# Norm sums and rows in one product each, and the mLSTM's diagonal and first states moved by a step

## The chip, the cores and the metric

The kernel runs on one core of a Trainium2 chip. The metric is the device time of one execution in microseconds (us). The kernel before takes 884.66 us, the median of three runs (884.0 to 885.25).

## The reference

One layer of a hybrid encoder on 512 tokens of 1024 channels, with 256 memory tokens, in float32:

```python
h = rms_norm(x, mix_norm_g)                      # y = x * rsqrt(mean(x*x) + EPS) * g
proj = h @ w_in                                  # mLSTM q,k,v,o,gates | NA q,k,v | memory q | merge gates
y_ml = mlstm_branch(...)                         # 4 heads of 128, chunkwise, forward and backward scans
y_na = neighbourhood_attention(...)              # 8 heads of 64 on an 8 x 64 grid
mem_k, mem_v = split(rms_norm(mem, mem_norm_g) @ w_mem_kv)
y_xa = memory_cross_attention(...)               # 4 heads of 128
merged = g_ml*(y_ml @ w_br_ml) + g_na*(y_na @ w_br_na) + g_xa*(y_xa @ w_br_xa)
x = x + merged @ w_out
a, u = split(rms_norm(x, ffn_norm_g) @ w_ffn_up) # ConvGLU, 2816 wide
x = x + (gelu(dwconv3(a)) * u) @ w_ffn_down
out = rms_norm(x, final_norm_g)
```

## The kernel before

Channels lie on the partitions and tokens along the free axis, so a projection of 128 output channels is a 128x512 tile that sums over 8 input tiles (k = 0 to 7). A float32 factor is kept as a high part in fp32r and a low part (the remainder), and `mm3` issues three products for each k: high x high, high x low, low x high (L203 to L205). A projection (`proj`) is therefore 24 products into one PSUM bank; `at={k: f}` lets it call `f` after the products of that k. Weights come in by `wr` loads on SP (L151), and ACT and DVE split them (L185, L186) ahead of their use. All engines work through their own instructions in order.

The norm factors `1/rms` are applied after the projections. The sum of squares of a token runs over partitions, so it is a product with a matrix of ones (`onesr`). `rstd_parts` splits the squares into a high and a low part (ACT L209, DVE L210); `rstd_cols` multiplies each by the ones into one bank (two products, L291), takes the diagonal of each 128 columns (L295) and raises it to -1/2 on POOL (L298). That gives a column `rc`: one number for each token, on partitions. `rstd_row` makes the same numbers a row `rb` on all partitions: the column, split in high and low (L300, L301), scales the identity (L306, one for each 128 tokens and part), and two products with the ones (L314) spread it. This happens for the norm of x, of the memory ("m", 256 tokens) and of the FFN ("2"); the final norm has no row.

The mLSTM is a generator whose pieces are put between the projections by hand: each `yield` hands back to the projections, which resume it once or twice a projection. Its start (`ml_prep`) makes gates, scans, a small diagonal matrix `dg` (L544) that spreads the scans' maxima (L551), and the tables `R` (loaded by SP from DRAM at L576; `load_R` also adds a mask on DVE, L579, giving `rm`). For a head, `begin` transposes keys (L598, L600) and scales them (ACT L602, DVE L604), `middle` computes the chunk states (L641, copied at L644 and combined at L646) and the first half of the decay matrices (`diagonal`: ACT exponentials of `rm` at L614, DVE L618), `rest` the second half, and `last` the weighted queries (L628, L630) and `load_R` of the next head. `values_J` (L657, L659) gives the outputs of a head in four parts, with the next head's `begin`, `middle`, `rest` and `last` behind them.

The projections around the first head are mLSTM's o0 to o3 (bank read by DVE L976, ACT L977, DVE L980), then the memory's keys and values. The memory norm's sums are issued in o2 after k=3, its row in the first key projection. In the FFN, `ua` and `uu` are the two halves of the up-projection; the sums of norm 2 are issued in `ua1`, its row behind it.

Of the kernel before, what the change touches and what calls it, by code (L numbers as in the profile page):

```python
# [11 lines left out]
F32 = mybir.dt.float32  # L12
F32R = mybir.dt.float32r
AF = mybir.ActivationFunctionType
ALU = mybir.AluOpType
AX = mybir.AxisListType

P = 128
S = 512
D = 1024  # L20
# [82 lines left out]
def hybrid_block(ctx, tc, xT, memT, wflat, vecs, gbias, nabias, outa, outb):  # L103
    nc = tc.nc
    V, A, G, PE, SY = nc.vector, nc.scalar, nc.gpsimd, nc.tensor, nc.sync

    cp = ctx.enter_context(tc.tile_pool(name="cp", bufs=1))
    wp = ctx.enter_context(tc.tile_pool(name="wp", bufs=3))
    up = ctx.enter_context(tc.tile_pool(name="up", bufs=NU))
    sp = ctx.enter_context(tc.tile_pool(name="sp", bufs=7))  # L110
    tp = ctx.enter_context(tc.tile_pool(name="tp", bufs=2))
# [6 lines left out]
    def nm(s):  # L118
        uid[0] += 1
        return f"{s}_{uid[0]}"  # L120
# [4 lines left out]
    def scr(n=512):  # L125
        return sp.tile([P, 512], F32, tag="scr", name=nm("s"))[:, :n]

    def tiny(n):
        return tp.tile([P, 32], F32, tag="tiny", name=nm("y"), bufs=12)[:, :n]
# [4 lines left out]
    def atps():  # L134
        return atp.tile([P, 512], F32, tag="at", name=nm("at"))
# [71 lines left out]
    def split_act(h, l, src, scale=1.0):  # L207

        A.activation(h, src, AF.Copy, scale=scale)  # L209
        V.scalar_tensor_tensor(l, src, scale, h.bitcast(F32), op0=ALU.mult, op1=ALU.subtract)  # L210
# [40 lines left out]

    ident = cp.tile([P, P], F32, name="ident")
    make_identity(nc, ident)
    ones = cp.tile([P, P], F32, name="ones")
    G.memset(ones, 1.0)
    onesr = cp.tile([P, P], F32R, name="onesr")
# [4 lines left out]
    for d in range(2):  # L261
# [4 lines left out]
                        pattern=[[sgn, P]], channel_multiplier=-sgn)  # L266
        msk.append(m)
    pads = []
    for i in range(2):
        t = cp.tile([P, 514], F32, name=f"pad{i}")  # L270
# [8 lines left out]

    def rstd_parts(acc, ntok):  # L280

        h, l = [sp.tile([P, 512], F32R, tag="scr", name=nm("s"))[:, :ntok] for _ in range(2)]
        split_act(h, l, acc)
        return h, l

    def rstd_cols(parts, ntok, tag, n=D):

        nt = ntok // P
        ps = atps()
        for i, part in enumerate(parts):  # L290
            PE.matmul(ps[:, :ntok], onesr, part, start=i == 0, stop=i == 1)  # L291
        v = tiny(nt)
        d = scr(P)
        for t in range(nt):
            V.tensor_tensor_reduce(d, ps[:, t * P:(t + 1) * P], ident, 1.0 / n, EPS, ALU.mult, ALU.add,  # L295
                                   accum_out=v[:, t:t + 1])
        col = cp.tile([P, nt], F32, name=f"rc_{tag}")
        G.tensor_tensor(col, v, nhalf[:, :nt], op=ALU.pow)  # L298
        ch, cl = tp.tile([P, 32], F32R, tag="tiny", name=nm("y"), bufs=12)[:, :nt], tiny(nt)
        A.activation(ch, col, AF.Copy)  # L300
        V.tensor_tensor(cl, col, ch.bitcast(F32), op=ALU.subtract)  # L301
        dgs = []
        for c in (ch.bitcast(F32), cl):
            dg = sp.tile([P, 512], F32R, tag="scr", name=nm("s"))[:, :ntok]
            for t in range(nt):
                V.tensor_scalar(dg[:, t * P:(t + 1) * P], ident, c[:, t:t + 1], None, op0=ALU.mult)  # L306
            dgs.append(dg)
        return col, dgs

    def rstd_row(dgs, ntok, tag):  # L310

        pb = atps()
        for n, dg in enumerate(dgs):
            PE.matmul(pb[:, :ntok], onesr, dg, start=n == 0, stop=n == 1)  # L314
        rb = cp.tile([P, ntok], F32, name=f"rb_{tag}", tag=f"rb{ntok}", bufs=2 if ntok == S else 1)
        A.activation(rb, pb[:, :ntok], AF.Copy)
        return rb
# [3 lines left out]
    XH = [hx[k // 4][:, (k % 4) * S:(k % 4 + 1) * S] for k in range(KT)]  # L321
    XL = [hx[2 + k // 4][:, (k % 4) * S:(k % 4 + 1) * S] for k in range(KT)]
    acc = cp.tile([P, S], F32, name="acc_x", tag="acc", bufs=1)
# [19 lines left out]
    norm = []  # L343

    def proj(key, XHs, XLs, n=S, bank=None, at={}):
        ws = weights(key)
        ps = (bank or mmps)()
        for k in range(KT):
            mm3(ps[:, :n], ws[k][0], ws[k][1], XHs[k], XLs[k], k == 0, k == KT - 1)
            if k in at:  # L350
                at[k]()
        return ps
# [3 lines left out]
    for k in range(KT):  # L356
# [6 lines left out]
        for f in range(4):  # L363
            fs = slice(f * P, (f + 1) * P)
            mm3(ps_q[f], wh[:, fs], wl[:, fs], XH[k], XL[k], k == 0, k == KT - 1)

    xp = rstd_parts(acc, S)
    ps_k = [proj(("mlk", 0), XH, XL, bank=atps, at={3: lambda: norm.append(rstd_cols(xp, S, "x"))}),
            proj(("mlk", 1), XH, XL, bank=atps, at={3: lambda: norm.append(rstd_row(norm[0][1], S, "x"))})]
    (rc, _), rb = norm  # L370
    rcc = cp.tile([P, NT], F32, name="rcc")
    V.tensor_scalar(rcc, rc, C_ML, None, op0=ALU.mult)
# [22 lines left out]
    for f in range(4):  # L395
        ps = ps_k[f] if f < 2 else proj(("mlk", f), XH, XL)
# [42 lines left out]
    for c, n in enumerate(TMW):  # L439
# [9 lines left out]
        for t in range(NT):  # L449
            ps = pss[t]  # L450
# [21 lines left out]
    ml = {}  # L472


    def ml_prep(load_R):
        gv = Gt.rearrange("p t (d k h) -> p t d k h", d=2, k=2)
        T4 = lambda a: a.rearrange("p (t d h) -> p t d h", t=4, d=2)
        f = tiny(32)
# [50 lines left out]
        dg = cp.tile([P, 4, NT, 4], F32, name="dg")  # L529
# [4 lines left out]
        for d in range(2):  # L534
            G.dma_start(rd[d], rr[32 * d:32 * d + 4, :])
        ml["rd"] = rd
        yield
        ml["R"] = load_R(0)
        for d in range(2):
            for u in range(2):  # L540
                g = 2 * u + d
                gs = slice(32 * g, 32 * g + 4)
                ends = mr[gs].rearrange("p (t c) -> p t c", t=NT)[:, :, P - 1 if d == 0 else 0:][:, :, 0:1]
                V.tensor_tensor(dg[gs, g], ends.to_broadcast([4, NT, 4]),  # L544
                                ident[gs, gs].unsqueeze(1).to_broadcast([4, NT, 4]), op=ALU.mult)
        pm = atps()
        pmv = pm[:, :400].rearrange("p (t c) -> p t c", t=NT)
        for t in range(NT):
# [20 lines left out]
    def ml_all():  # L569
# [125 lines left out]
        def begin(h):  # L695
            kt, C = own(h)
            st_[h] = dict(kt=kt, C=C, kq=keys(h, kt), R=ml.pop("R"))
# [14 lines left out]
                ml["R"] = load_R(h + 1)  # L712

        begin(0)
        yield
        middle(0)
        yield
# [4 lines left out]
        for h in range(4):  # L722
            x = st_.pop(h)
# [242 lines left out]
    for f in range(4):  # L966
        ps = proj(("xaq", f), XH, XL, at=mid())
# [3 lines left out]
    for f in range(4):  # L971
# [3 lines left out]
        t = scr()  # L975
# [26 lines left out]
    for f in range(4):  # L1002
        ps = proj(("naq", f), XH, XL, at=mid())
        V.tensor_tensor(nq[:, f * S:(f + 1) * S].rearrange("p (b r c) -> p b r c", r=ROWS, b=4), rv(ps), rv(rb),
                        op=ALU.mult)
# [201 lines left out]
    for hh in range(2):  # L1207
        gu = [unit(F32R) for _ in range(6)]
        UH = [gu[k // 4][:, (k % 4) * S:(k % 4 + 1) * S] for k in range(HF)]
        UL = [gu[3 + k // 4][:, (k % 4) * S:(k % 4 + 1) * S] for k in range(HF)]  # L1210
        for j in range(HF):
            f = HF * hh + j
            if f == 0:
                wa, wu = weights(("ua", f)), weights(("uu", f))
                pa, pu = mmps(), mmps()
                for k in range(KT):
                    if k < KT - 1:
                        mm3(pa, wa[k][0], wa[k][1], HH[k], HL[k], k == 0, False)
                for k in range(KT - 1):
                    mm3(pu, wu[k][0], wu[k][1], HH[k], HL[k], k == 0, False)  # L1220
                p2 = rstd_parts(acc2, S)
                k = KT - 1
                mm3(pa, wa[k][0], wa[k][1], HH[k], HL[k], False, True)
                mm3(pu, wu[k][0], wu[k][1], HH[k], HL[k], False, True)
            else:
                pa = pa1 if f == 1 else proj(("ua", f), HH, HL)
            if f == 0:
                pa1 = proj(("ua", 1), HH, HL, at={0: lambda: norm.append(rstd_cols(p2, S, "2"))})
                rb2 = rstd_row(norm[4][1], S, "2")
            c = conv(pa, rb2, "ffw", "ffb", f, FT)  # L1230
            sq = scr()
            A.activation(sq, c, AF.Square)
            V.scalar_tensor_tensor(sq, sq, GC, c, op0=ALU.add, op1=ALU.mult)  # L1233
            A.activation(sq, sq, AF.Tanh, scale=GK)  # L1234
            V.scalar_tensor_tensor(c, sq, 1.0, c, op0=ALU.add, op1=ALU.mult)  # L1235
            G.tensor_tensor(c, c, rb2, op=ALU.mult)  # L1236
            if f > 0:
                pu = proj(("uu", f), HH, HL)
            V.tensor_tensor(c, pu, c, op=ALU.mult)  # L1239
            split_act(UH[j], UL[j], c, 0.5)  # L1240
        for f in range(KT if hh == 0 else LF - 1):
            ws = weights(("dn", hh, f, 0)) + weights(("dn", hh, f, 1))
            ps = mmps()
            for k in range(HF):
                mm3(ps, ws[k][0], ws[k][1], UH[k], UL[k], k == 0, k == HF - 1)
            V.tensor_tensor(x2[f], ps, x2[f], op=ALU.add)
            if hh == 1:
                if f == 0:
                    A.activation(acc3, x2[f], AF.Square)
                else:  # L1250
                    sq = scr()
                    A.activation(sq, x2[f], AF.Square)
                    G.tensor_tensor(acc3, acc3, sq, op=ALU.add)
                A.activation(x2[f], x2[f], AF.Copy, scale=vcol("fin_g", f))
        if hh == 1:
            last_tiles(UH, UL)
# [107 lines left out]
```

## Time and profile before

| | |
|---|---|
| median of three runs | 884.66 us (884.0 to 885.25) |
| the profiled execution | 883.28 us, of which the span is 881.5 us |
| instructions | 12183 |
| PE busy | 874.1 us, 4330 products |
| DVE, ACT, POOL busy | 581.7, 449.7, 136.0 us |
| granted TensorE clock, mean | 0.999 |

Rows of a timeline give start and duration in us, then engine, line, operation, out<-in and shape; "xN" joins N instructions in a row, and a bracket at the end gives the idle time before and what ended it. Rows of groups give busy time and the mean duration of one in ns. Matmuls are pipelined, so the distance from one start to the next tells what a product takes of PE, and the duration is longer. The queue on SP issues DMAs.

### The profile page before, as it was taken

What the parts mean: (1) busy time and instruction counts of PE and PEld (TensorE: products, weight loads), DVE (VectorE), ACT (ScalarE), POOL (GpSimd) and SP (SyncE); (2) the same over time, 40 slices, a digit from 0 to 9 for tenths busy, and PEclk for the clock granted to TensorE, in tenths of its full rate; (3) what the DMA queues carried; (4) which work ended last, traced back from release to release, by engine and by line L of the source; (5) the groups of instructions that cost most, each with busy time, mean ns of one, the idle gap of its engine ahead of it and who ended that gap; (6) DMA issues with size and microseconds to landing.
All of it is one profiled execution on the core that took longest, in us unless ns stands there. A gap on an engine that the chain in (4) does not pass through costs nothing.

```text
span 881.5 us, 12183 instructions
## 1 busy us (share of the span) xinstructions
PE 874.1 (99%) x4330; PEld 741.3 (84%) x4330; DVE 581.7 (66%) x1196; ACT 449.7 (51%) x958; POOL 136.0 (15%) x215
## 2 busy tenths in 40 slices
PE   9999999999999999999999999999999999999997
PEld 7898889988888888888888888888888888888897
DVE  6694688775576648988676557676633466667433
ACT  7363457664355538888644435544422344444532
POOL 1001100000004900642000212111100011111010
PEclk9999999999999999999999999999999999999999
DMA  8224544522223533545323432322233333332412
GB/s 273 88 83 135 183 150 132 145 95 96 73 95 99 139 101 116 150 140 167 96 96 109 143 108 80 112 96 95 75 99 104 106 98 98 99 101 78 141 33 96
DMA packets 39436, 99.67 MB, mean 113 GB/s; under 512 B 5960, under 2 KB 13640, under 8 KB 39376
## 3 DMA queue, kind: packets, MB, share of 16 engines
q1 hardware_dynamic: 31728, 92.45, 32.5%
q0 software_dynamic: 7360, 6.32, 3.2%
q8 instruction: 34, 0.56, 0.3%
q14 instruction: 26, 0.21, 0.1%
q10 hardware_dynamic: 288, 0.14, 0.1%
HBM read 94.67 MB, written 4.21 MB: 112 GB/s over the span
## 4 chain that ended last, share of the span: by engine, by line
PE 97%; DVE 1%; issue 1%; ACT 0%; POOLq 0%; POOL 0%; DVEq 0%; ACTq 0%
PE mm L203 28%; PE mm L204 28%; PE mm L205 28%; PE at L203 2%; PE at L205 2%; PE at L204 2%; PE at L820 1%; PE at L657 1%; PE at L801 1%; PE at L641 1%; PE at L659 1%; PE at L782 0%; PE at L783 0%; PE at L235 0%; PE at L598 0%
## 5 line engine op out<-in xcount | busy, mean ns | idle before, releaser
L203 PE MATMUL mm<-u,w 128*128 128x512 f32 (+1 forms) x1077 | 417.7, 388 | 0.0
L205 PE MATMUL mm<-u,w 128*128 128x512 f32 (+1 forms) x1077 | 414.0, 384 | 0.0
L204 PE MATMUL mm<-u,w 128*128 128x512 f32 (+1 forms) x1077 | 413.9, 384 | 0.0
L185 ACT ACTIVATE w<-wr 128x512 fp32r<-128x512 f32 (+1 forms) x298 | 184.6, 623 | 233.5 <-PE mm L205 201.1
L186 DVE TENSOR_TENSOR w<-wr,w 128x512 fp32r<-128x512 f32 (+3 forms) x299 | 207.4, 695 | 108.6 <-ACT w L185 106.5
L205 PEld LDWEIGHTS mm<-u,w 128*128 128x128 f32 x1077 | 202.5, 188 | 41.1 <-DVE w L186 0.7
L203 PEld LDWEIGHTS mm<-u,w 128*128 128x128 f32 x1077 | 202.7, 188 | 39.3 <-ACT w L185 0.6
L204 PEld LDWEIGHTS mm<-u,w 128*128 128x128 f32 x1077 | 202.7, 188 | 38.9 <-DVE u L210 0.5
L468 POOL DMA_DIRECT2D u<-nav_d x128 | 62.3, 522 | 108.0 <-PE at L820 63.1
L1236 POOL TENSOR_TENSOR s<-s,rb 128x512 f32<-128x512 f32 x22 | 37.5, 1703 | 250.0 <-DVE s L1235 250.0
L209 ACT ACTIVATE u<-s 128x512 fp32r<-128x512 f32 x26 | 16.4, 632 | 55.3 <-DVE s L1239 54.5
L1239 DVE TENSOR_TENSOR s<-mm,s 128x512 f32<-128x512 f32 x22 | 15.2, 690 | 23.4 <-POOL s L1236 23.4
L382 ACT ACTIVATE s<-pad,vec 128x512 f32<-128x512 f32 x30 | 24.4, 812 | 6.9 <-DVE pad L380 6.3
L210 DVE SCALAR_TENSOR_TENSOR u<-s,u 128x512 fp32r<-128x512 f32 x26 | 18.0, 691 | 14.6 <-ACT u L209 14.4
L383 DVE SCALAR_TENSOR_TENSOR s<-pad,vec,s 128x512 f32<-128x512 f32 x30 | 22.5, 750 | 4.1 <-ACT s L382 4.1
L1082 POOL TENSOR_TENSOR acc<-acc,s 128x512 f32<-128x512 f32 x7 | 9.1, 1296 | 102.9 <-ACT s L1081 102.9
L1235 DVE SCALAR_TENSOR_TENSOR s<-s,s 128x512 f32<-128x512 f32 x22 | 15.2, 692 | 14.0 <-ACT s L1234 14.0
L384 DVE SCALAR_TENSOR_TENSOR s<-pad,vec,s 128x512 f32<-128x512 f32 x30 | 22.5, 750 | 0.8
L1234 ACT ACTIVATE s<-s 128x512 f32<-128x512 f32 x22 | 13.9, 632 | 16.3 <-DVE s L1233 16.2
L203 PE MATMUL mm<-w,u 128*128 128x512 f32 x48 | 19.0, 396 | 0.0
L205 PE MATMUL mm<-w,u 128*128 128x512 f32 x48 | 18.7, 390 | 0.0
L204 PE MATMUL mm<-w,u 128*128 128x512 f32 x48 | 18.7, 389 | 0.0
(288 smaller groups left out, 1008.5 us busy)
## 6 DMA issues: line engine op xcount, KB each, us to landing
wr<-wflat SPq DMA_DIRECT2D x140, 512.0 KB, 3.3
s<-xT SPq DMA_DIRECT2D x16, 256.0 KB, 4.5
nab<-nabias SPq DMA_DIRECT2D x16, 256.0 KB, 2.6
u<-nav_d POOLq DMA_DIRECT2D x128, 32.0 KB, 2.5
wr<-wflat SPq DMA_DIRECT2D x15, 192.0 KB, 2.4
nav_d<-nv POOLq DMA_DIRECT2D x8, 256.0 KB, 2.8
R<-rd SPq DMA_DIRECT2D x8, 256.0 KB, 3.5
wr<-wflat SPq DMA_DIRECT2D x2, 544.0 KB, 3.4
```

Of the source, the lines that this page charges most:

```text
L185: A.activation(h[:, u:v], src, AF.Copy)
L186: V.tensor_tensor(l[:, u:v], src, h[:, u:v].bitcast(F32), op=ALU.subtract)
L203: PE.matmul(ps, lh, rh, start=start, stop=False)
L204: PE.matmul(ps, lh, rl, start=False, stop=False)
L205: st["mm"] = PE.matmul(ps, ll, rh, start=False, stop=stop).ins
L209: A.activation(h, src, AF.Copy, scale=scale)
L210: V.scalar_tensor_tensor(l, src, scale, h.bitcast(F32), op0=ALU.mult, op1=ALU.subtract)
L382: A.activation(t1, pad[:, 0:512], AF.Identity, scale=vcol(w, i), bias=vcol(b, i))
L383: V.scalar_tensor_tensor(t1, pad[:, 1:513], vcol(w, n + i), t1, op0=ALU.mult, op1=ALU.add)
L384: V.scalar_tensor_tensor(t1, pad[:, 2:514], vcol(w, 2 * n + i), t1, op0=ALU.mult, op1=ALU.add)
L468: G.dma_start(vw[r * 32:(r + 1) * 32, i * 256:(i + 1) * 256], nav_v[hf, r, CW[b]:CW[b] + 32, hp * 256:(hp + 1) * 256])
L1236: G.tensor_tensor(c, c, rb2, op=ALU.mult)
```

## The change

Three things are changed.

1. **High and low on one contraction.** `rstd_parts` first adds the upper 64 partitions of the squares to the lower 64 (ACT copies them down, DVE adds), then writes the high part into partitions 0 to 63 of one tile and the low part into 64 to 127. One product with the ones then sums both. For the row, the diagonal holds the high part and a swapped identity (`swap`, ones at a distance of 64 partitions) adds the low part of the token 64 partitions away, so that one product suffices there too. The products move: for x one k later at both places, for the FFN from k=0 to k=2 of `ua1`, and its row from behind `ua1` into `uu1` after k=1, for which `uu1` is issued ahead of the rest of f=0.
2. **The diagonal.** `dg` (L544, L550 after) is made ahead of the `yield` and of `load_R(0)` instead of behind them.
3. **The idle step.** One more `yield` stands between `begin(0)` and `middle(0)`, so everything from the first states on is shifted by a step.

```diff
+    swap = cp.tile([P, P], F32, name="swap")
+    G.memset(swap, 0.0)
+    for i in (-64, 64):
+        G.affine_select(out=swap, in_=swap, compare_op=ALU.not_equal, fill=1.0, base=i, pattern=[[-1, P]],
+                        channel_multiplier=1)
...
     def rstd_parts(acc, ntok):
-        h, l = [sp.tile([P, 512], F32R, tag="scr", name=nm("s"))[:, :ntok] for _ in range(2)]
-        split_act(h, l, acc)
-        return h, l
+        t = scr(ntok)
+        both = sp.tile([P, 512], F32R, tag="scr", name=nm("s"))[:, :ntok]
+        A.activation(t[:64], acc[64:128], AF.Copy)
+        V.tensor_tensor(t[:64], t[:64], acc[:64], op=ALU.add)
+        A.activation(both[:64], t[:64], AF.Copy)
+        V.tensor_tensor(both[64:128], t[:64], both[:64].bitcast(F32), op=ALU.subtract)
+        return both
...
-        for i, part in enumerate(parts):
-            PE.matmul(ps[:, :ntok], onesr, part, start=i == 0, stop=i == 1)
+        PE.matmul(ps[:, :ntok], onesr, both, start=True, stop=True)
...
+        A.activation(cs[:64], cl[64:128], AF.Copy)
+        A.activation(cs[64:128], cl[:64], AF.Copy)
+        dg = sp.tile([P, 512], F32R, tag="scr", name=nm("s"))[:, :ntok]
+        for t in range(nt):
+            ts = slice(t * P, (t + 1) * P)
+            V.tensor_scalar(dg[:, ts], ident, ch[:, t:t + 1].bitcast(F32), None, op0=ALU.mult)
+            V.scalar_tensor_tensor(dg[:, ts], swap, cs[:, t:t + 1], dg[:, ts].bitcast(F32), op0=ALU.mult, op1=ALU.add)
...
-        for n, dg in enumerate(dgs):
-            PE.matmul(pb[:, :ntok], onesr, dg, start=n == 0, stop=n == 1)
+        PE.matmul(pb[:, :ntok], onesr, dg, start=True, stop=True)
...
-    ps_k = [proj(("mlk", 0), XH, XL, bank=atps, at={3: lambda: norm.append(rstd_cols(xp, S, "x"))}),
+    ps_k = [proj(("mlk", 0), XH, XL, bank=atps, at={4: lambda: norm.append(rstd_cols(xp, S, "x"))}),
...
-        yield
-        ml["R"] = load_R(0)
         for d in range(2):
             for u in range(2):
...
                 V.tensor_tensor(dg[gs, g], ends.to_broadcast([4, NT, 4]),
                                 ident[gs, gs].unsqueeze(1).to_broadcast([4, NT, 4]), op=ALU.mult)
+        yield
+        ml["R"] = load_R(0)
...
         begin(0)
+        yield
         yield
         middle(0)
...
-                pa1 = proj(("ua", 1), HH, HL, at={0: lambda: norm.append(rstd_cols(p2, S, "2"))})
-                rb2 = rstd_row(norm[4][1], S, "2")
+                pa1 = proj(("ua", 1), HH, HL, at={2: lambda: norm.append(rstd_cols(p2, S, "2"))})
+                pu1 = proj(("uu", 1), HH, HL, at={1: lambda: norm.append(rstd_row(norm[4][1], S, "2"))})
+                rb2 = norm[5]
...
-                pu = proj(("uu", f), HH, HL)
+                pu = pu1 if f == 1 else proj(("uu", f), HH, HL)
```

After the change L291 is L299, L314 is L322, L544 is L550, L551 is L559, L579 is L587, L604 is L612, L641 is L649, L646 is L654, L630 is L638, L976 is L985 and L980 is L989.

On PE, at the first states of the mLSTM: before, they follow o0 (mm_1295) and o1 (mm_1354) comes behind them.

```order
609 L204 MATMUL mm_1295<-u_153,w_1199 128x512
610 L205 MATMUL mm_1295<-u_151,w_1199 128x512
611 L641 MATMUL at_1325<-u_581,u_1270 128x129 x3
612 L641 MATMUL at_1332<-u_581,u_1270 128x129 x3
613 L203 MATMUL mm_1354<-u_150,w_1289 128x512
```

After, they follow o1 (mm_1343), and o2 (mm_1407) comes behind them, with the memory norm's sums (L299) after its first twelve products.

```order
632 L205 MATMUL mm_1343<-u_159,w_1302 128x512
633 L649 MATMUL at_1372<-u_591,u_1280 128x129 x3
634 L649 MATMUL at_1379<-u_591,u_1280 128x129 x3
635 L203 MATMUL mm_1407<-u_158,w_1337 128x512
636 L204 MATMUL mm_1407<-u_160,w_1337 128x512
```

The states have moved behind one more projection, and only 12 products now lie between them and the memory's sums.

On PE, at the memory norm's sums before, in o2 (mm_1420): head 0's first values (L657, L659) and head 1's transposes (L598, L600) stand ahead of them.

```order
646 L657 MATMUL at_1432<-u_581,E_1339 128x129 x2
647 L659 MATMUL at_1432<-u_1270,E_1395 128x129
648 L598 MATMUL at_1445<-u_445,u_446 128x128 x4
649 L600 MATMUL at_1446<-ident,u_446 128x128 x4
650 L203 MATMUL mm_1420<-u_150,w_1348 128x512
651 L204 MATMUL mm_1420<-u_152,w_1348 128x512
652 L205 MATMUL mm_1420<-u_150,w_1348 128x512
653 L291 MATMUL at_1464<-s_1408,onesr 128x256
```

After, those have moved into o3.

```order
644 L203 MATMUL mm_1407<-u_158,w_1337 128x512
645 L204 MATMUL mm_1407<-u_160,w_1337 128x512
646 L205 MATMUL mm_1407<-u_158,w_1337 128x512
647 L299 MATMUL at_1445<-s_1394,onesr 128x256
648 L203 MATMUL mm_1407<-u_159,w_1340 128x512
```

The values and transposes are no longer ahead of the sums.

On DVE, at the operand of the memory norm's sums before (L210, s_1409): R_1402 and R_1406 are the masked tables of head 1, mm_1354 is o1.

```order
182 L630 TENSOR_TENSOR E_1390<-E_1390,u_445 128x384
183 L646 SCALAR_TENSOR_TENSOR u_1270<-u_1270,ex,at_1332 128x129
184 L630 TENSOR_TENSOR E_1395<-E_1395,u_445 128x384
185 L579 TENSOR_TENSOR R_1402<-R_1400,msk_130 128x512
186 L186 TENSOR_TENSOR w_1414<-wr_1287,w_1414 128x512
187 L976 TENSOR_TENSOR s_1379<-mm_1354,rb_x 128x512
188 L579 TENSOR_TENSOR R_1406<-R_1404,msk_135 128x512
189 L210 SCALAR_TENSOR_TENSOR s_1409<-acc_m,s_1408 128x256
```

After, the operand's last step is L292 (s_1394), and R_1436 is head 1's first masked table.

```order
181 L587 TENSOR_TENSOR R_1436<-R_1434,msk_138 128x512
182 L638 TENSOR_TENSOR E_1429<-E_1429,u_455 128x384
183 L186 TENSOR_TENSOR w_1401<-wr_1297,w_1401 128x512
184 L985 TENSOR_TENSOR s_1368<-mm_1343,rb_x 128x512
185 L186 TENSOR_TENSOR w_1404<-wr_1297,w_1404 128x512
186 L290 TENSOR_TENSOR s_1393<-s_1393,acc_m 64x256
187 L989 TENSOR_SCALAR u_1333<-s_1368 128x512
188 L654 SCALAR_TENSOR_TENSOR u_1280<-u_1280,ex,at_1372 128x129
189 L654 SCALAR_TENSOR_TENSOR u_1280<-u_1280,ex,at_1379 128x129
190 L654 SCALAR_TENSOR_TENSOR u_1280<-u_1280,ex,at_1372 128x129
191 L654 SCALAR_TENSOR_TENSOR u_1280<-u_1280,ex,at_1379 128x129
192 L292 TENSOR_TENSOR s_1394<-s_1393,s_1394 64x256
```

The four combining steps of the states (L646, L654 after) have moved from ahead of the masked tables to behind the first of them, and the operand's last step stands behind them.

More of the change, by code (lines that the diff above doesn't have):

```diff
@@ L280, in rstd_parts, with rstd_cols @@
     def rstd_parts(acc, ntok):
-        h, l = [sp.tile([P, 512], F32R, tag="scr", name=nm("s"))[:, :ntok] for _ in range(2)]
-        split_act(h, l, acc)
-        return h, l
-    def rstd_cols(parts, ntok, tag, n=D):
+        t = scr(ntok)
[5 more added lines that the diff above has]
+        return both
+    def rstd_cols(both, ntok, tag, n=D):
         nt = ntok // P
         ps = atps()
-        for i, part in enumerate(parts):
-            PE.matmul(ps[:, :ntok], onesr, part, start=i == 0, stop=i == 1)
+        PE.matmul(ps[:, :ntok], onesr, both, start=True, stop=True)
         v = tiny(nt)
@@ L298, in rstd_cols, with rstd_row @@
         G.tensor_tensor(col, v, nhalf[:, :nt], op=ALU.pow)
-        ch, cl = tp.tile([P, 32], F32R, tag="tiny", name=nm("y"), bufs=12)[:, :nt], tiny(nt)
+        ch, cl, cs = tp.tile([P, 32], F32R, tag="tiny", name=nm("y"), bufs=12)[:, :nt], tiny(nt), tiny(nt)
         A.activation(ch, col, AF.Copy)
         V.tensor_tensor(cl, col, ch.bitcast(F32), op=ALU.subtract)
[L302 to L310, printed above, removed]
+        A.activation(cs[:64], cl[64:128], AF.Copy)
[5 more added lines that the diff above has]
+            V.scalar_tensor_tensor(dg[:, ts], swap, cs[:, t:t + 1], dg[:, ts].bitcast(F32), op0=ALU.mult, op1=ALU.add)
+        return col, dg
+    def rstd_row(dg, ntok, tag):
         pb = atps()
-        for n, dg in enumerate(dgs):
-            PE.matmul(pb[:, :ntok], onesr, dg, start=n == 0, stop=n == 1)
+        PE.matmul(pb[:, :ntok], onesr, dg, start=True, stop=True)
         rb = cp.tile([P, ntok], F32, name=f"rb_{tag}", tag=f"rb{ntok}", bufs=2 if ntok == S else 1)
@@ L367, in hybrid_block @@
     xp = rstd_parts(acc, S)
-    ps_k = [proj(("mlk", 0), XH, XL, bank=atps, at={3: lambda: norm.append(rstd_cols(xp, S, "x"))}),
-            proj(("mlk", 1), XH, XL, bank=atps, at={3: lambda: norm.append(rstd_row(norm[0][1], S, "x"))})]
+    ps_k = [proj(("mlk", 0), XH, XL, bank=atps, at={4: lambda: norm.append(rstd_cols(xp, S, "x"))}),
+            proj(("mlk", 1), XH, XL, bank=atps, at={4: lambda: norm.append(rstd_row(norm[0][1], S, "x"))})]
     (rc, _), rb = norm
```

## The prediction

> **What bounds the kernel now.** I read the page first, then the waits of PE, then PE's timeline at each place that the change touches, and last the queues of DVE and ACT around the places where PE will arrive at another time.
>
> ```profile
> span 881.5 us, 12183 instructions
> PE 874.1 (99%) x4330; PEld 741.3 (84%) x4330; DVE 581.7 (66%) x1196; ACT 449.7 (51%) x958; POOL 136.0 (15%) x215
> PE 97%; DVE 1%; issue 1%; ACT 0%; POOLq 0%; POOL 0%; DVEq 0%; ACTq 0%
> PE at L235 <- DVE warm L231: 1.2, 1, 1.2
> PE at L641 <- ACT u L602: 0.4, 1, 0.4
> PE at L551 <- DVE dg L544: 0.2, 1, 0.2
> 589.81 0.39 PE L203 MATMUL mm<-u,w 128*128 128x512 f32 x1
> 590.04 0.39 PE L204 MATMUL mm<-u,w 128*128 128x512 f32 x1
> ```
>
> PE is busy 99% of the span and carries 97% of the chain that ended last, so time comes or goes only as products on PE are removed or as PE is made to wait. The waits listed for PE (total, times, longest) are one at the start and two inside the mLSTM, 0.6 us together. In undisturbed stretches one 128x512 product follows another at 590.04 - 589.81 = 0.23 us (0.2267 us from four in a row: the rows are rounded). The profiled execution took 883.28 us, 1.8 us more than its span; the median of the three runs is 884.66 us. I add the sum to 883.28 and shift it by the 1.38 us between the two.
>
> **The six ones-products.** Six products against the matrix of ones go (two each for the norms of x, memory and the FFN, one at the sums, one at the row).
>
> ```profile
> L314 PE MATMUL at<-s,onesr 128*128 128x512 f32 x4 | 1.2, 389 | 0.0
> L291 PE MATMUL at<-s,onesr 128*128 128x512 f32 x4 | 1.2, 389 | 0.0
> L314 PE MATMUL at<-s,onesr 128*128 128x256 f32 x2 | 0.4, 283 | 0.0
> L291 PE MATMUL at<-s,onesr 128*128 128x256 f32 x2 | 0.4, 280 | 0.0
> 138.49 0.40 PE L291 MATMUL at<-s,onesr 128*128 128x256 f32 x2
> 138.72 0.40 PE L203 MATMUL mm<-u,w 128*128 128x512 f32 x1
> ```
>
> Half of each group goes: four of 128x512 and two of 128x256. The 389 ns is latency; what the next product waits is the spacing, 0.227 us, and for 256 columns (138.72 - 138.49)/2 = 0.12 us. That is 4 x 0.227 + 2 x 0.12 = **-1.15 us**, all on the path. The Trainium skill ("TensorE: Matmul & The Clock Gate", on why the gap is 56 ns) gives 215.7 ns for a product of 512 columns; by it the term would be an estimated -1.08. The measured spacing decides.
>
> **The diagonal a step sooner.** L544 moves ahead of the yield, so `dg` no longer stands behind what DVE does for the step between.
>
> ```profile
> 114.85 0.51 PE L549 MATMUL at<-ident,s 100*128 100x100 f32 x4
> 115.52 0.41 PE L551 MATMUL at<-dg,ones 100*128 100x64 f32 x2 [0.16 <-DVE dg L544]
> ```
>
> Before, PE goes from L549's start to L551's in 0.67 us; the four need 4 x 0.09 = 0.35 us by their own rows. With `dg` ready early, **-0.32 us**. Nothing comes in its place: the transposes' own inputs are older.
>
> **The idle step.** The first states (L641) move behind one more projection of 24 products.
>
> ```profile
> 126.06 0.69 PE L641 MATMUL at<-u,u 128*128 128x129 f32 x4
> 127.12 1.32 PE L641 MATMUL at<-u,u 128*128 128x129 f32 x8 [0.37 <-ACT u L602]
> 128.20 0.48 PE L203 MATMUL mm<-u,w 128*128 128x512 f32 x1
> 144.40 1.50 PE L641 MATMUL at<-u,u 128*128 128x129 f32 x12
> 145.66 0.48 PE L203 MATMUL mm<-u,w 128*128 128x512 f32 x1
> ```
>
> The twelve passes take 128.20 - 126.06 = 2.14 us here and 1.26 us at the second head: 0.88 us is lost. Later by 24 x 0.2267 = 5.44 us, the key tiles (last one ready at about 127.5 before) lie 3 us early, so all of it goes: **-0.88 us**. The price is that every mLSTM piece after it falls one step later, among other work.
>
> **What the idle step uncovers.** The memory norm's sums (L291, after L299) stand where they stood, in projection o2, but PE now comes there sooner: the values of head 0 and the transposes of head 1, ahead of it before, now stand behind it. PE's arrival: 126.06 - 0.45 (two x-norm products) - 0.32 + 5.44 + 1.33 (states, twelve passes of 0.111) + 12 x 0.2267 = **134.8**, against 138.49. Its operand does not move along:
>
> ```profile
> 129.66 0.33 SPq L576 DMA_DIRECT2D R<-rd  x1
> 132.39 0.37 SPq L576 DMA_DIRECT2D R<-rd  x1
> DMA to landing us min/median/max: 3.1/3.5/4.7
> 128.66 1.27 ACT L614 ACTIVATE E<-R,bi 128x128 f32<-128x128 f32 x4
> 132.14 0.60 DVE L646 SCALAR_TENSOR_TENSOR u<-u,ex,at 128x129 f32<-128x129 f32 x2
> 133.39 0.55 DVE L630 TENSOR_TENSOR E<-E,u 128x384 f32<-128x384 f32 x1
> 133.86 0.69 DVE L579 TENSOR_TENSOR R<-R,msk 128x512 f32<-128x512 f32 x1
> 134.46 0.69 DVE L186 TENSOR_TENSOR w<-wr,w 128x512 fp32r<-128x512 f32 x1
> 135.06 0.69 DVE L976 TENSOR_TENSOR s<-mm,rb_x 128x512 f32<-128x512 f32 x1
> 135.96 0.69 DVE L579 TENSOR_TENSOR R<-R,msk 128x512 f32<-128x512 f32 x1 [0.21 <-DMA R<-rd]
> 136.57 0.42 DVE L210 SCALAR_TENSOR_TENSOR s<-acc_m,s 128x256 fp32r<-128x256 f32 x1
> 136.90 0.42 DVE L980 TENSOR_SCALAR u<-s 128x512 f32<-128x512 f32 x1
> 137.24 0.68 DVE L186 TENSOR_TENSOR w<-wr,w 128x512 fp32r<-128x512 f32 x1
> ```
>
> Before, the low part (L210) is done at 136.99, 1.5 us before PE wants it. Afterwards the last step of the stacked operand (L292) is the twelfth instruction on DVE from the mask of head 1's R (L587), which waits for its DMA. That DMA waits until ACT's exponentials have read the old masked tile: 129.66 before, at the end of the third of the four L614. Without the stalled key tiles ahead of them I put it at about 128.5. Landing at the median 3.5 gives 132.0. From there, by the distance between starts in the rows above: mask 0.60, L638 0.47, three of L186 and L985 at 0.60, L290 0.33, L989 0.34, four L654 at 0.26 (two take 0.60, one 0.35), L292 0.42: 5.0 us, so 137.0. PE waits 137.0 - 134.8 = **+2.2 us**. Behind the waiting product on PE stand the rest of o2 and everything else, so all of it is span. Ends: landing at 3.1, and the DMA and DVE's queue 0.9 earlier together, as the work ahead of them starts earlier too, give 0.9; landing at 4.7 gives 3.4. I keep 2.2: the issues at 129.66 and 132.39 had their masks 4.2 and 3.6 us later, so the median of 3.5 is no long landing.
>
> **The longer way to sums and rows.** The operand now takes four half-height steps, ACT and DVE in turn, instead of two; the diagonal takes one tensor_scalar and one scalar_tensor_tensor for each 128 columns, and two tiny ACT copies more. For x and the FFN norm PE's own products cover this, or just fail to.
>
> ```profile
> 522.92 0.61 PE L291 MATMUL at<-s,onesr 128*128 128x512 f32 x2
> 523.71 0.28 DVE L295 CUSTOM_DVE_ANT_0 s<-at,ident 128x128 f32<-128x128 f32 x1
> 525.08 1.03 POOL L298 TENSOR_TENSOR rc<-y,nhalf 128x4 f32<-128x4 f32 x1 [7.88 <-DVE y L295]
> 526.46 1.65 DVE L306 TENSOR_SCALAR s<-ident,y 128x128 fp32r<-128x128 f32 x8
> 528.13 0.62 PE L314 MATMUL at<-s,onesr 128*128 128x512 f32 x2
> ```
>
> FFN norm: the sums move from k=0 to k=2, six products later, to 522.92 + 1.36 = 524.28. L295 began 0.57 after its last product (523.14), and 2.75 after that DVE began the diagonals: 524.28 + 0.57 + 2.75 = 527.6. Eight tensor_scalars took 1.65 (0.20 each); four of them and four scalar_tensor_tensors (0.25 to 0.26, from the pair of L646) take about 1.85, so the row's operand is ready at 529.45 to 529.55. The row stands 22 products behind the sums, at 524.28 + 22 x 0.2267 = 529.26: **+0.28 us** of waiting (0 to 0.5). x norm: both products move by one k together, 24 slots apart as before, and by the same lengths the diagonal is ready 0.1 us ahead of the row: **+0.05** (0 to 0.2). The FFN's second up-projection now runs ahead of f=0's square and gate on ACT; they come some 1.6 us later, and only their own tile waits for them, since the next bank is freed by the second `pad`: 0, and the 1.6 us would count only if a bank hung on it. `swap`, two selects on POOL at the start, lies more than 20 us ahead of its first use: 0. R's loads change places with weight loads on SP; a weight load behind a waiting R is late by up to 2 us, and its data are wanted a projection (5.4 us) later: 0.
>
> **Later heads.** Their pieces stand beside other projections than before. Before, one of the four heads still loses the 0.4 us that the list of waits shows (at 190 us). It may vanish (-0.4), or a stall like that of the first states may come (+0.9). I take 0.
>
> **Sum.** -1.15 - 0.32 - 0.88 + 2.2 + 0.28 + 0.05 = **+0.2 us**: 883.5 us for a profiled execution, **884.9 us** as a median.
>
> **Rivals.** About 0.2%, 1.8 us, is what a measurement of this kernel can tell from no change.
>
> *The memory sums do not wait.* If R lands early, or ACT's exponentials are through two microseconds sooner, L292 meets PE and the first sum stands without its fourth term: -2.0 us, 882.6 us, faster by 0.23%. For it: 1.5 us of slack before, and that everything ahead on PE comes 0.8 us sooner. Against it: the queue above must shrink from 5.0 + 3.5 us to 6.3.
>
> *The memory sums wait long enough to slow the clock.* Slower, by one mechanism:
>
> ```profile
> 1.19 3.57 PE L235 MATMUL at<-warm 128*128 128x256 f32 x15 [1.19 <-DVE warm L231]
> ```
>
> After the idle start fifteen products of 256 columns take 3.57 us, 0.24 us apiece against 0.12 later: PE ran at half pace for its first 3.6 us. If the stop at the memory sums sets it back so, PE loses about 15 x 0.12 = 1.8 us more. With a wait of 3.4 us (the landing at 4.7) that is -2.0 + 3.4 + 1.8 = +3.2 us, 887.8 us. From what wait on it decides the trace does not show, only that it is above 0.4 us: after its later waits the products keep their spacing. The Trainium skill (the same page, on the HAM clock gate) puts it at an idle window of about 3.4 us. By that rule a wait of 2.2 us is free and one at my upper end is at the edge; the trace agrees on the half pace after the idle start.
>
> *The later heads and the row of the FFN pay.* Two stalls of 0.9 us among heads 1 to 3 and 0.5 at the row, with the memory wait at 2.2: +2.2 us, 886.9 us.
>
> **How the numbers follow.** The forecast (a memory wait of 0.9 to 3.4 us, later heads -0.4 to +0.9) has 0.66 and by itself spans 883.1 to 886.9; of it 0.52 lies within 0.2%, 0.05 below and 0.09 above. No memory wait: 0.19. Slowed clock: 0.07. Later heads and row: 0.08. Leaving out the clock and a little at either end, the range is 882.3 to 887.1. Faster: 0.19 + 0.05 = 0.24; slower: 0.09 + 0.07 + 0.08 = 0.24; within: 0.52.
>
> **What would show it.** In the new profile the list of PE's waits should hold L299 <- DVE s L292 with about 2 us, and no wait at L559 (the old L551) or at the first L649. L292 should come after L587, which idles for the DMA of R. L299 and L322 should have half the count of L291 and L314. At the FFN row PE should wait about 0.3 us. The prediction is wrong if L299 shows no wait (then near 882.6), or if PE's products of the step after it run at twice their spacing.

## The result and the profile after

The changed kernel takes 887.48 us (median of 7 runs) against 884.45 us of the kernel before beside it: a ratio of 1.0035, with a 95% interval from 1.0021 to 1.0049. It is slower, by 3 us. Six of the seven runs lie between 886.78 and 888.38 us at a mean granted clock (the share of full TensorE speed that the chip allowed) of 0.995 to 0.997; the seventh took 882.97 us at 0.999. That spread is part of the answer.

The page of the changed kernel's profiled execution, which took 888.38 us, begins:

```profile
span 886.6 us, 12195 instructions
```

Its list of PE's waits (engine, line and what it waited for: us in total, times, longest):

```profile
PE at L299 <- DVE s L292: 4.2, 1, 4.2
PE at L235 <- DVE warm L231: 1.2, 1, 1.2
PE mm L204 <- DVE u L210: 0.3, 1, 0.3
PE at L322 <- DVE s L316: 0.2, 1, 0.2
PE mm L203 <- ACT w L185: 0.2, 1, 0.2
```

The two waits in the mLSTM are gone, and one of 4.2 us at the memory norm's sums (L299) stands in their place. (The waits at L204 and L203 are at 5.6 and 8.6 us, at the start of the kernel.) PE's timeline at that stop, with the last product ahead of it:

```profile
130.93 1.50 PE L649 MATMUL at<-u,u 128*128 128x129 f32 x12
132.18 0.47 PE L203 MATMUL mm<-u,w 128*128 128x512 f32 x1
...
134.76 0.39 PE L205 MATMUL mm<-u,w 128*128 128x512 f32 x1
139.34 0.58 PE L299 MATMUL at<-s,onesr 128*128 128x256 f32 x1 [4.20 <-DVE s L292]
139.72 0.63 PE L203 MATMUL mm<-u,w 128*128 128x512 f32 x1
140.15 0.63 PE L204 MATMUL mm<-u,w 128*128 128x512 f32 x1
...
144.42 0.51 PE L205 MATMUL mm<-u,w 128*128 128x512 f32 x1
144.77 0.40 PE L203 MATMUL mm<-u,w 128*128 128x512 f32 x1
145.00 0.40 PE L204 MATMUL mm<-u,w 128*128 128x512 f32 x1
```

PE was at the sums at 134.99 (the start of the product before, 134.76, and 0.23) and went on at 139.34, a stop of 4.35 us; the list counts 4.20, from the end of that product. The twelve products behind follow one another at 140.15 - 139.72 = 0.43 us, nearly twice the usual 0.23, and from 144.77 on at 0.23 again. They take 5.05 us instead of 2.72, and L299 itself 0.38 instead of 0.12: 2.6 us more than the stop's 4.35. The table of stretches for the changed kernel (window; length; busy us of PE, PEld, DVE, ACT and POOL, with counts; the granted clock; DMA share; GB/s) shows the same as a clock:

```profile
130.00:135.00 5.00, 5.00 (x29) 4.16 (x27) 3.74 (x9) 4.97 (x14) 0.00 (x0) 1.00 0.56 147
135.00:140.00 5.00, 0.80 (x3) 0.66 (x3) 4.94 (x13) 1.91 (x6) 0.00 (x0) 0.78 0.54 175
140.00:145.00 5.00, 5.00 (x13) 3.86 (x13) 2.36 (x12) 0.61 (x3) 1.11 (x1) 0.54 0.00 1
145.00:150.00 5.00, 5.00 (x32) 4.44 (x31) 2.63 (x7) 2.66 (x8) 0.00 (x0) 1.00 0.34 108
```

What the sums waited for begins on SP, with the first R load of head 0 and the first of head 1:

```profile
119.28 0.33 SPq L584 DMA_DIRECT2D R<-rd  x1
...
130.50 0.33 SPq L584 DMA_DIRECT2D R<-rd  x1
```

and goes on on DVE, with the masks on them and the end of the queue behind the second:

```profile
123.03 0.69 DVE L587 TENSOR_TENSOR R<-R,msk 128x512 f32<-128x512 f32 x1 [2.69 <-DMA R<-rd]
...
134.18 0.69 DVE L587 TENSOR_TENSOR R<-R,msk 128x512 f32<-128x512 f32 x1 [0.86 <-DMA R<-rd]
...
137.06 0.41 DVE L290 TENSOR_TENSOR s<-s,acc_m 64x256 f32<-64x256 f32 x1
137.39 0.41 DVE L989 TENSOR_SCALAR u<-s 128x512 f32<-128x512 f32 x1
137.73 1.11 DVE L654 SCALAR_TENSOR_TENSOR u<-u,ex,at 128x129 f32<-128x129 f32 x4
138.87 0.42 DVE L292 TENSOR_TENSOR s<-s,s 64x256 fp32r<-64x256 f32 x1
```

DVE stands idle for R before each of the two masks, and L292 ends at 139.29, 0.05 us ahead of L299.

Between the profiled executions the span grew by 886.6 - 881.5 = 5.1 us. Comparing starts on PE stretch by stretch, it comes together like this: -1.15 for the products, -0.34 at the diagonal, +6.24 between 120 and 160 us (the stop and the slow products, 6.95, less the 0.88 of the stall at the first states; some 0.2 is spread over small pieces), +0.2 at the x norm's row, +0.5 at the FFN's row, -0.35 at the last head's states, whose old loss of 0.4 us (at 190 us in before) is gone. The medians differ by 3.0 us only: the profiled execution of before was a quick one (883.28 us against a median of 884.45), that of the changed kernel a long one (888.38 against 887.48).

### The profile page after: what moved, and what is told of

The parts are those of the page before. It is cut to its first block, busy times and chain, and to the rows that moved or that the text cites. A ratio compares the mean times of both kernels' runs of the same rounds, so it can differ in the third digit from the quotient of the medians.

```text
span 886.6 us, 12195 instructions
## 1 busy us (share of the span) xinstructions
PE 874.8 (99%) x4324; PEld 741.3 (84%) x4324; DVE 586.2 (66%) x1199; ACT 453.6 (51%) x967; POOL 136.5 (15%) x218
## 4 chain that ended last, share of the span: by engine, by line
PE 92%; issue 2%; DMA 2%; DVE 2%; ACT 1%; POOL 0%; SPq 0%; POOLq 0%; DVEq 0%; ACTq 0%
PE mm L203 27%; PE mm L205 27%; PE mm L204 27%; PE at L203 2%; PE at L205 2%; PE at L204 2%; PE at L829 1%; DMA R<-rd 1%; PE at L665 1%; PE at L810 1%; PE at L667 1%; DMA wr<-wflat 1%; DMA rd<-s 1%; PE at L649 0%; PE at L791 0%
## 5 line engine op out<-in xcount | busy, mean ns | idle before, releaser
L203 PE MATMUL mm<-u,w 128*128 128x512 f32 (+1 forms) x1077 | 418.3, 388 | 0.2 <-ACT w L185 0.2
L204 PE MATMUL mm<-u,w 128*128 128x512 f32 (+1 forms) x1077 | 414.6, 385 | 0.3 <-DVE u L210 0.3
L203 PEld LDWEIGHTS mm<-u,w 128*128 128x128 f32 x1077 | 203.1, 189 | 39.6 <-ACT w L185 0.6
L204 PEld LDWEIGHTS mm<-u,w 128*128 128x128 f32 x1077 | 203.1, 189 | 39.4 <-DVE u L210 0.6
L210 DVE SCALAR_TENSOR_TENSOR u<-s,u 128x512 fp32r<-128x512 f32 x26 | 17.9, 690 | 13.5 <-ACT u L209 13.3
L203 PE MATMUL mm<-w,u 128*128 128x512 f32 x48 | 19.0, 395 | 0.0
L204 PE MATMUL mm<-w,u 128*128 128x512 f32 x48 | 18.7, 390 | 0.0
```

Source lines behind the costliest of these rows:

```text
L203: PE.matmul(ps, lh, rh, start=start, stop=False)
L204: PE.matmul(ps, lh, rl, start=False, stop=False)
```

## The experiments

All edits are to the changed kernel unless "before" is named; each set ran beside runs of before on its chip.

**The changed kernel again.** No edit.

> The changed kernel itself once more, beside the others of this set. Theory: a stop of about 4 us at L299 and a slow stretch behind it in most executions, mean clock 0.995 to 0.997, about 3 us above before. An execution whose R lands early stays at 0.999 and is no slower than before. Rival (the slow clock has nothing to do with the stop): executions with a low clock appear as often in the kernels without the stop.

886.72 us against 884.19, ratio 1.0034 (1.0021 to 1.0046), all five runs at a clock of 0.995 to 0.997. PE at the stop in its profile:

```profile
138.50 0.58 PE L299 MATMUL at<-s,onesr 128*128 128x256 f32 x1 [3.79 <-DVE s L292]
138.88 0.63 PE L203 MATMUL mm<-u,w 128*128 128x512 f32 x1
...
141.44 0.52 PE L203 MATMUL mm<-u,w 128*128 128x512 f32 x1
141.80 0.40 PE L204 MATMUL mm<-u,w 128*128 128x512 f32 x1
142.03 0.39 PE L205 MATMUL mm<-u,w 128*128 128x512 f32 x1
```

The stop is 3.8 us here and the slow stretch 3.3 us, against 4.2 and 5.4: both vary from one execution to the next. In the 27 runs of before beside them the lowest clock is 0.997, twice; five of them took 885.8 to 886.8 us, and no trace shows why. None of the five runs of the changed kernel was a quick one, so its run of 882.97 us, and whether R landed early in it, stays without a trace.

**Sums two and four k later.** The stop is made shorter, the operand left as it is.

```diff
-        ps = proj(("o", f), XH, XL, at=mid({3: lambda: norm.append(rstd_cols(mp, M, "m"))} if f == 2 else {}))
+        ps = proj(("o", f), XH, XL, at=mid({5: lambda: norm.append(rstd_cols(mp, M, "m"))} if f == 2 else {}))
```

> The changed kernel with the memory norm's sums two k later in o2, six products of 0.227 us. Theory: the same operand, so the wait falls from 4.2 to about 2.9 us, under the length that slows the clock; the products behind it keep 0.227 us and the clock 0.999: 885.6 us. Rival (any stop of microseconds slows the clock): the twelve products behind run at 0.43 us and the time is about 888 us.

884.65 us against 883.49, ratio 1.0014 (1.0006 to 1.0023), about 1 us better than expected. The profile has a stop of 1.9 us and no slow stretch:

```profile
138.31 0.39 PE L299 MATMUL at<-s,onesr 128*128 128x256 f32 x1 [1.93 <-DVE s L292]
138.53 0.39 PE L203 MATMUL mm<-u,w 128*128 128x512 f32 x1
138.76 0.39 PE L204 MATMUL mm<-u,w 128*128 128x512 f32 x1
```

The stop is shorter than the 2.9 us expected because R landed sooner in this execution: L292 ended at 138.25, against 139.29 and 138.44 in the two profiles above. A new wait of 0.5 us stands at the memory's row (L322). Moving six products (1.36 us) took 1.8 us off the loss by the ratios and 1.4 to 1.9 by the medians, so the times alone do not tell whether more than the move itself came back; that the slow stretch is gone is seen in the trace. Three of its eleven runs still have a clock of 0.996. With k=5 the stop may at times be long enough, but none of the three has a trace.

The same with k=7:

> The changed kernel with the memory norm's sums at k=7 of o2, twelve products (2.7 us) later. Theory: the stop falls to at most 1.5 us, no execution shows a clock under 0.998, and what the sums no longer wait for is found in part further back, at the memory row's bank and at the second head's states, 1 to 2 us: 883.5 to 884.5 us, level with before. Rival (each k gained is time gained): 1.2 us under the kernel with k=5 and below before.

884.46 us against 884.19, ratio 1.000 (0.9991 to 1.0008), and no run under 0.998. The stop is 1.6 us, only 0.3 less than with k=5, because R landed 0.9 us later in this execution; and the wait at the memory norm's row has grown to 1.5:

```profile
PE at L299 <- DVE s L292: 1.6, 1, 1.6
PE at L322 <- DVE u L654: 1.5, 1, 1.5
```

**The operand earlier.** The opposite cure: PE comes when it comes, and L290 to L292 are issued ahead of o1, so that on DVE they stand ahead of the mask of head 1's R.

```diff
-        if f == 2:
+        if f == 1:
             mp = rstd_parts(macc, M)
```

> The changed kernel with the memory norm's stacked operand issued one projection earlier, ahead of o1 instead of o2; on DVE its last step L292 then stands ahead of the mask of head 1's R. Theory: no wait at L299, clock 0.999, all the savings are left and only the 0.5 to 0.6 us at the rows of x and the FFN against them: 882.7 us, 0.998 of before. Rival (the shifted mLSTM pieces or the longer sums cost): 886 to 887 us with the losses elsewhere.

883.74 us against 883.49, ratio 1.0002 (0.9993 to 1.0011). The stop is gone (L299 at 134.98, its operand at 133.7), the clock is 0.998 to 0.999 in every run, and nearly 3 us come back. But the time is level with before, where I had expected 0.998. PE's waits tell why:

```profile
PE at L322 <- DVE u L654: 1.5, 1, 1.5
PE at L649 <- ACT u L610: 0.8, 2, 0.6
PE at L322 <- DVE s L316: 0.2, 1, 0.2
```

PE now runs ahead into the second head: its states wait for key tiles, and the memory's row (L322) waits 1.5 us for the combining of those states (L654), which must read its bank before the row may write one. The operand of L322 had been ready for over 9 us.

**The idle step alone, on before.**

```diff
         begin(0)
         yield
+        yield
         middle(0)
```

> The kernel before with the idle step alone. Theory: the 0.9 us at the first states goes, and the sums of the memory norm (L291) wait for L210, which stands only five places behind the mask instead of eleven: a wait of 1.0 to 1.8 us, clock 0.999, 884.6 to 885.4 us. Rival (the idle step alone brings the loss): a wait of 4 us, a slow clock and 887 to 888 us.

883.54 us against 883.49, ratio 0.9997 (0.9989 to 1.0006), clock 0.998 to 1.000. The list of waits has L291 with 1.6 us:

```profile
PE at L291 <- DVE s L210: 1.6, 1, 1.6
PE at L314 <- DVE u L646: 0.3, 1, 0.3
```

The time is below the 884.6 to 885.4 us expected. The idle step takes the stall at the first states away, as it should, and loses about as much again at the sums and the row: 1.6 and 0.3 us, against a stall of 0.9 us in the profiled execution of before and of 1.7 where R comes at its usual time (see below). Most of the way from 1.6 to the 4 us of the whole change is the stacked operand: L292 stands six places farther back on DVE than L210 and ends 5.1 us after the start of the mask instead of 137.17 - 133.87 = 3.3. PE's earlier arrival gives another 0.5, a later R 0.3, and the length of the stop brings the clock in. Neither half alone shows the loss of the whole.

**Without the idle step, and the norms alone.** First, the extra `yield` taken out of the changed kernel; second, before with the norms alone (the diagonal, too, as before).

> The changed kernel without the idle step. Theory (a stop at the memory norm's sums, long enough that PE's clock falls): values and transposes stand ahead of the sums again, PE comes there at about 137.7 us, and L292 should end at 138.3 to 139.1, so a wait of 0.5 to 1.4 us is left, the clock stays at 0.999, and the stall of 0.9 us at the first states comes back: 884.1 to 885.0 us. Rival (the longer way to sums and rows costs by itself, wherever it stands): as slow as the whole change, about 887 us.

883.78 us against 883.49, ratio 1.0005 (0.9997 to 1.0014). One of the eleven runs, of 885.17 us, has a clock of 0.996 and no trace; the others have 0.998 to 1.000.

> The kernel before with the stacked norms alone, the mLSTM as before. Theory (the chain from the scans over R to the key tiles sets the pace at 100 to 150 us, whatever PE saves ahead of it): the 0.23 us saved at x is given back at the first states, whose stall grows from 0.9 by about as much, the rows of x and the FFN cost 0.2 and 0.5 us, and the six products are worth nothing on balance: within 0.5 us of before, clock 0.999. Rival (the savings stand, only the idle step hurts): 1.1 us faster than before.

883.99 us against 884.19, ratio 0.9995 (0.9986 to 1.0004). PE's timeline at the first states, without the idle step and then with the norms alone:

```profile
125.33 0.38 PE L649 MATMUL at<-u,u 128*128 128x129 f32 x2
127.11 0.49 PE L649 MATMUL at<-u,u 128*128 128x129 f32 x2 [1.40 <-ACT u L610]
127.97 1.32 PE L649 MATMUL at<-u,u 128*128 128x129 f32 x8 [0.37 <-ACT u L610]
```

```profile
126.13 0.38 PE L649 MATMUL at<-u,u 128*128 128x129 f32 x2
127.17 0.49 PE L649 MATMUL at<-u,u 128*128 128x129 f32 x2 [0.66 <-ACT u L610]
128.03 1.32 PE L649 MATMUL at<-u,u 128*128 128x129 f32 x8 [0.37 <-ACT u L610]
```

PE arrives 0.8 us sooner in the first, and the key tiles come at 127.1 and 128.0 in both: what was saved ahead of this place, the diagonal's third of a microsecond and in this execution a quicker start, is waited off here. The wait that I expected at L299 without the idle step did not come (L299 stood at 139.36, its operand at 139.2); the stall at the first states held PE back instead.

**Three operands given time.** The early operand, the memory's row at k=7 of its projection, and the FFN's sums at k=1.

```diff
-        if f == 2:
+        if f == 1:
             mp = rstd_parts(macc, M)
...
-        ps = proj(("memk", f), MH, ML, M, at={3: lambda: norm.append(rstd_row(norm[2][1], M, "m"))} if f == 0 else {})
+        ps = proj(("memk", f), MH, ML, M, at={7: lambda: norm.append(rstd_row(norm[2][1], M, "m"))} if f == 0 else {})
...
-                pa1 = proj(("ua", 1), HH, HL, at={2: lambda: norm.append(rstd_cols(p2, S, "2"))})
+                pa1 = proj(("ua", 1), HH, HL, at={1: lambda: norm.append(rstd_cols(p2, S, "2"))})
```

> The changed kernel with three operands given time: the memory norm's operand one projection earlier, its row at k=7 of the first key projection instead of k=3 (twelve products of 0.12 us, 1.4 us later), and the FFN's sums at k=1 (the row 3 products farther behind them). Theory: of the early-operand kernel's losses the 1.5 us at the memory row nearly go, and the 0.4 us at the FFN's row, while 0.8 us at the second head's states stay: 1.5 to 1.8 us less than that kernel, 0.998 of before, about 882 us. Rival (the mLSTM chain sets the pace and takes the time back at the next place where PE meets it): the wait appears at the next values or states and the time is level with before.

882.08 us against 884.19, ratio 0.9979 (0.9970 to 0.9988): faster than before, and faster than the change as it was made. PE's whole list of waits:

```profile
PE at L235 <- DVE warm L231: 1.2, 1, 1.2
PE at L649 <- ACT u L610: 0.9, 2, 0.6
```

and the groups of two kinds of ones-products (busy us, mean ns of one, idle time before):

```profile
L322 PE MATMUL at<-s,onesr 128*128 128x512 f32 x2 | 0.9, 428 | 0.0
L299 PE MATMUL at<-s,onesr 128*128 128x256 f32 x1 | 0.3, 277 | 0.0
```

No ones-product waits any more, and between the medians there are 2.1 us, close to the -2.0 of the prediction's first rival. The agreement is in part luck: the FFN's row no longer pays 0.5 us, the second head's states pay 0.9, and the stall that was taken away is larger in most executions than in the one that was priced. Between the two profiled executions the gain is 881.5 - 880.6 = 0.9 us.

## Why the prediction was wrong

The forecast of 884.9 us, within 0.2%, was wrong. What happened is its second rival, a stop long enough to slow the clock, with 887.8 us and a chance of 0.07. The mechanism of the likeliest case was right, a stop at the sums with R's transfer and DVE's queue behind it, and the size of its fourth term was not. That 887.8 lies so near the measured 887.48 is in part luck: the stop was longer than the rival's 3.4 us, and other parts made up for it.

**The terms that held.** The ones-products left 12 and came to 6. L559 has no wait, 0.34 us against 0.32. The first states run through, 130.93 against a forecast of 130.7. PE arrived at the sums at 134.99 against 134.8. From the mask to the end of L292 the queue took 139.29 - 134.18 = 5.1 us against 5.0.

**The term that failed: +2.2 us for the memory sums' wait.** The step is the one that put the issue of head 1's R "at about 128.5", 1.2 us ahead of where the trace of before has it, because the stalled key tiles no longer stood ahead of it. Here is the last key tile on ACT, in before and in the changed kernel:

```profile
126.70 0.37 ACT L602 ACTIVATE u<-at,ex 128x128 f32<-128x128 f32 x1 [0.49 <-DVE u L604]
127.54 0.37 ACT L610 ACTIVATE u<-at,ex 128x128 f32<-128x128 f32 x1 [0.49 <-DVE u L612]
```

The key tiles stand ahead of ACT's exponentials in both kernels, and what they wait for is DVE, not PE. The chain begins with head 0's R, in before:

```profile
117.95 0.33 SPq L576 DMA_DIRECT2D R<-rd  x1
122.19 0.69 DVE L579 TENSOR_TENSOR R<-R,msk 128x512 f32<-128x512 f32 x1 [1.79 <-DMA R<-rd]
```

In before, the issue of head 1's R follows this mask by 129.66 - 122.19 = 7.47 us; in the changed kernel by 130.50 - 123.03 = 7.47 us, and in the other eight profiles by 7.46 to 7.48, whether the first states stall or not. So the chain from that mask over the key tiles and ACT's exponentials does not care when PE takes the tiles. The stall was PE waiting for this chain, not holding it up.

The rest, 0.84 us, is that head 0's R came later, though its tables were sent sooner. In the profiled execution of before SP issued that load at 117.95; in the nine other profiles, with the mLSTM's order of before or the new one, it lies between 118.66 and 119.35. Why is not shown. The one profile from which I read the chain had an early one, and I took it for the rule. With the changed kernel's 3.75 us from that load to its mask, 7.47 from there, 3.7 for the landing and 5.1 for the queue, loads at 118.66 to 119.35 put the stop at 3.7 to 4.4 us; the two profiles have 3.95 and 4.35 from PE's arrival on. My upper end for it was 3.4. Nor would a landing at the forecast 132.0 alone have been enough: DVE idled only 0.86 us ahead of the mask, since L638 before it ended at 133.32.

The early R also made the stall at the first states look small. In the profile of the norms alone PE came at 126.13, as in before, R's load was issued at 119.35, and the twelve passes took 0.84 us longer: a stall of 1.7 us instead of 0.88. That fits the quick profiled execution of before, but no second trace of before shows it.

**The clock.** Priced at 1.8 us from the start of the kernel, it cost 2.6 in one profile and 1.6 in the other. I had it at 0.07 since the stop I forecast was below the length at which I took it to act. When the clock fell can be read from short stretches, one of the changed kernel's first profile and one of its second:

```profile
137.50:138.00 0.50, 0.00 (x0) 0.00 (x0) 0.50 (x3) 0.50 (x3) 0.00 (x0) 0.82 0.00 0
138.00:138.50 0.50, 0.00 (x1) 0.01 (x1) 0.45 (x2) 0.00 (x0) 0.00 (x0) 0.79 0.94 369
```

A mean of 0.82 over 0.5 us, with full clock ahead and half behind, means half clock from 137.82 on; the second gives 138.29. PE had come to the sums at 134.99 and 134.55, so the clock fell 2.8 and 3.7 us into the stop. It came back at 144.65 and 141.70, after 6.8 and 3.4 us. Stops of 1.9 and 1.6 us were followed by no slow products. The Trainium skill ("TensorE: Matmul & The Clock Gate", on the HAM clock gate) puts the fall at an idle window of about 3.4 us; the second profile agrees, the first does not, with 2.8 us, and the measurement decides. Whether a stop between 1.9 and 2.8 us can bring the fall is not shown, and the runs with k=5 at 0.996 have no trace.

**The small terms.** The FFN's row was forecast at +0.28 (0 to 0.5) and cost 0.5: PE was held from 534.32 to 534.71, and the wait was 0.39, not 0.28: the operand was ready 5.2 us after the sums, as reckoned, but PE took it up 0.15 us later. The product behind the row and the next few lost another 0.1. The x row cost 0.2 against 0.05. The later heads, taken at 0, gave 0.35 back. The prediction had the 0.4 us at 190 us from the list of waits; the 0.4 us of the list is the wait at 127.12, inside the first states, and the last head's passes at 190.12 lost as much again in pieces that the list does not name.

**What the sum could not show.** Even with the right price the parts do not add. Alone, the idle step and the norms are each level with before (0.9997 and 0.9995), and with the diagonal's step they cost 0.35% together. Between 120 and 160 us a chain off PE sets when the operands are ready, and in every variant but the last the time that PE saved ahead of it was waited off at a later operand of that chain.

## What to carry to other kernels

When a stall is taken away by giving its operand time, list the next three or four operands that PE meets, and work out when each is ready on its own queue: moving PE earlier moves none of them that do not hang on PE. An operand's last step on a busy in-order engine belongs ahead of any instruction there that waits for a DMA; issuing it one projection sooner took back nearly 3 us here, though 1.5 us of new waiting then stood at the memory's row. A chain with a DMA in it should be timed from several executions, and a stop that may reach a few microseconds should be priced with the slow products behind it.

## What the runs showed of the hardware

- After a stop of 4 us PE ran at 0.43 us a product of 512 columns instead of 0.23, for 5.4 us in one execution and 3.3 us in another. The clock fell 2.8 and 3.7 us into these stops and stayed at half for 6.8 and 3.4 us.
- The half pace at the start of the kernel (0.24 us for 256 columns, as the mean of fifteen) stands under a recorded clock of 1.00, the one at 140 us under 0.54: the record did not show the first. The stretch at the start, in the changed kernel:

```profile
0.00:5.00 5.00, 3.78 (x16) 3.46 (x16) 0.86 (x3) 2.47 (x4) 4.31 (x27) 1.00 0.53 141
```

- In all ten profiles the clock is at half in the last 0.9 to 3.7 us too, behind the last product. That alone gives a mean clock of 0.998 to 1.000; a spell of 3.4 us in the middle takes another 0.002. The two runs of before at 0.997 and the one without the idle step at 0.996 may have had such a spell; they have no trace.
- Half the partitions are not half the time: L290 and L292 on 64 partitions took 0.41 and 0.42 us, as L210 did on 128. Stacking therefore doubled the steps on ACT and DVE at full price.
